# T1 made in GLA's loop, the last quarter summed block by block in the attention, and another order of the output projection's products, PSUM chains and transfers

## The chip, the cores and the metric

The kernel runs on one core of one Trainium2 chip. The metric is the device time of one execution in microseconds; the median of three runs of the kernel before is 1924.75 us (1923.8 to 1924.92). Lower is better. Inputs and outputs are float32.

## What is computed

The reference is one decoder layer over 1024 tokens of width 1024, batch 1, followed by a final norm:

```python
x = x + 0.5 * swiglu_ffn(rmsnorm(x, ffn1_norm), ...)     # width 2816
x = x + hybrid_mixer(rmsnorm(x, mix_norm), w_in, ...)
x = x + 0.5 * swiglu_ffn(rmsnorm(x, ffn2_norm), ...)
return rmsnorm(x, final_norm)
```

The mixer makes one combined projection of the normed tokens and splits its columns between two groups of heads:

```python
o_nsa = nsa_attention(q, ...)          # 8 softmax heads: compressed, selected, window branches, gated
log_a = log_sigmoid(ga @ w_a2 + b_a) / GLA_TAU
o_gla = gla_attention(gq, gk, gv, log_a)     # 4 heads of gated linear attention, in chunks
o_gla = rmsnorm(o_gla, gla_g) * silu(gr)
return concatenate([o_nsa, o_gla], axis=-1) @ w_out
```

Only the way from `o_nsa` and `o_gla` to the product with `w_out`, and the addition of that product to x, is touched by the change.

## The kernel before

**Numbers.** Every large product is made from pairs: an operand is split into a rounded part and the rest, and `mm3` (L211 to L213) issues three matmuls for one product, high by high, high by low and low by high. Splitting takes one ScalarE copy (L206, L239) and one VectorE subtraction (L207, L248).

**Order.** The order of the work is written out by hand. Each engine runs its own list in program order, and so do the DMA queues: nearly all transfers are issued by SP, in the order of the program. Work beside the products is written as generators in `self.side`; `tick()` (L64) advances the first of them by one step, or fetches one pair of weights if some are owed (`later`). `block` (L945) is one product of four k tiles, twelve matmuls, with a tick behind each k tile. `fetch` takes a raw tile that a transfer on SP has filled (`raws`; three raw tiles) and lets ScalarE copy its high part; `settle` lets VectorE subtract.

**The mixer's stages** in the profiled execution: the combined projection until about 778 us; GLA's loop from 778 to 871; queries, keys and the scores of the compressed branch until 985; the attention until 1181; the output projection until 1272; then the second FFN.

**GLA's loop** (`gla`) has 8 iterations of 128 tokens. In each, `tm` issues the products of the gate's columns, `update`, `inter` and L1187 the products of the chunk. `finish(i)` then squares the chunk's output (L1119, ScalarE), reduces it (L1121), makes 1/rms (L1124 on GpSimd) and scales it (L1127, VectorE), which reads the two PSUM banks that L1187 of the next iteration writes. `out(i - 1)` transposes the block before (L1135, TensorE), copies it to a tile "hf" (L1138), stores it to the DRAM tensor gl (L1140), and for the second half of the tokens splits it (L206, L207) and stores both parts to og[1] (L1145). `out` stands ahead of `finish` in each iteration. There are two tiles "hf", which other work uses too: L1287 copies each finished query product into one, and stores it to DRAM (Qfd) from ScalarE's queue.

**The output projection** is one level of Strassen's scheme in Winograd's form. The columns of `w_out` and the tokens are halved, so that eight quarter products become seven, called 1 to 7, of four output tiles m each. The products' weights are quarters of `w_out` (1, 2, 4) or sums of quarters that the kernel has put into two DRAM tensors, `sums0` and `sums1`, while FFN1 ran (5, 3 and 7 with 6). The operands on the tokens' side are "11" and "12" (attention's rows of the first and second half of the tokens), "22" (GLA's rows of the second half) and four combinations of quarters:

- T1 is GLA's rows of the first half minus those of the second,
- T2 and T3 come from "11" and the GLA quarters,
- T4 comes from "12" and T2.

Before the change, `differences` makes T1 at the attention's start from gl (four loads, four GpSimd subtractions at L1494, four stores to DRAM tensor td) and, when the first half's attention is stored, T2 and T3. "22" is loaded ahead of the attention, and two output tiles of product 1 are computed early, between the attention's first units; `early` and `keep` hold them in PSUM and send them to the DRAM tensor part. In `prepare`, a side generator of the projection, the operands are loaded and split (`eased`, L2038 to L2040): T2 on VectorE, T1 and T3 on GpSimd, and T4 is computed there from "12" (L2020 to L2026).

The loop over `plan` in `run` then issues 26 blocks in the order 1 (two tiles), 3, 6, 5, 7, 2, 4. Products 1, 6 and 5 are added up in the same PSUM bank, and each block's sum is added to x by VectorE (L2368, `add`); `moved` lists sums of the early tiles, which GpSimd adds. x is first loaded from the DRAM tensor xs. `done` squares a finished tile and sends it to DRAM for the second FFN. When the last block of product 7 is added, the first half of the tokens is complete; `second` begins its norm: L276 adds up the squares, L287 is eight small matmuls that sum them over the partitions, L292 to L299 give 1/rms, and L324 scales x. Products 2 and 4 run beside it. `self.away` gives the four pairs of the ring of weights that the projection uses.

The attention runs over 88 units (`units`: query block, group, branch, heads). L1566 on GpSimd multiplies the softmax by the gates, L1587 transposes it on TensorE. `collect` sends each finished block of eight to og and counts it in `stored`.

## Time and profile before

The profiled execution took 1924.24 us, its span is 1922.5 us.

| stage | from to (us) | TensorE busy | granted clock | DMA share |
|---|---|---|---|---|
| GLA's loop, later part | 838 to 872 | 33.67 of 34 | 1.00 | 0.44 |
| start of the queries | 872 to 884 | 12.00 of 12 | 1.00 | 0.93 |
| attention | 985 to 1170 | 182.74 of 185 | 1.00 | 0.44 |
| projection, start | 1181 to 1197 | 15.04 of 16 | 1.00 | 0.94 |
| projection | 1197 to 1212 | 14.49 of 15 | 1.00 | 1.05 |
| projection | 1212 to 1237 | 18.43 of 25 | 0.96 | 0.51 |
| projection | 1237 to 1245 | 5.49 of 8 | 0.50 | 0.22 |
| projection, end | 1255 to 1272 | 17.00 of 17 | 0.99 | 0.48 |

PE is TensorE's matmuls, PEld its weight loads, DVE is VectorE, ACT ScalarE, POOL GpSimd, SP the engine that issues most transfers. A row of the waits reads: engine, bank, line that waited, the releasing instruction, then total us, how often, and the longest. A row of the timeline reads: start, duration, engine, line, operation, tile written and tiles read, and in brackets the idle time before it and what ended it. The table of stretches gives the busy time of each engine with the number of instructions, then the granted clock, the mean share of 16 DMA engines in use and GB/s; busy time is counted from records, some of which overlap.

### The profile page before, as it was taken

The page shows a single profiled execution, that of the slowest core. Times are in us where ns is not written, and L with a number is a line of the kernel's source. Part 1 is how long each engine was busy: PE and PEld are TensorE (multiplying, and loading weights), DVE is VectorE, ACT ScalarE, POOL GpSimd, SP SyncE. Part 2 cuts the span into 40 slices and gives each one's busy share as a digit, 9 for nine tenths or more (in the row PEclk, how much of TensorE's full clock was granted, in tenths as well). Part 3 has the DMA queues.
Part 4 walks back from the last instruction along what each step waited for, and adds up shares of the span by engine and source line. Part 5 has one row for each costly group of instructions (what it writes and reads, how often), then busy time and mean ns, then how long its engine had stood idle before and what let it go on. Part 6 is the DMA issues. An engine that isn't in the chain of part 4 may idle for free.

```text
span 1922.5 us, 26555 instructions
## 1 busy us (share of the span) xinstructions
PE 1891.8 (98%) x9243; PEld 1556.8 (81%) x9243; DVE 1414.3 (74%) x2319; ACT 898.8 (47%) x1723; POOL 283.3 (15%) x325
## 2 busy tenths in 40 slices
PE   9999999999999999999999999899999999999998
PEld 7888888888888888778887887678888888888887
DVE  7977778888876761554778887876777777767766
ACT  6633333344544551333488886345433333344343
POOL 0000000033000010121455752600000000000001
PEclk9999999999999999999999999899999999999999
DMA  7434455679964230129474525544333455688652
GB/s 261 154 130 142 141 187 213 225 273 387 376 219 157 88 109 20 44 62 264 159 240 121 173 72 177 199 160 171 116 125 126 154 197 197 217 295 299 233 172 88
DMA packets 182518, 343.37 MB, mean 179 GB/s; under 512 B 18640, under 2 KB 50512, under 8 KB 181872
## 3 DMA queue, kind: packets, MB, share of 16 engines
q1 hardware_dynamic: 171504, 318.31, 48.2%
q0 software_dynamic: 5024, 18.62, 2.7%
q10 hardware_dynamic: 5856, 4.75, 0.8%
q8 instruction: 73, 1.20, 0.3%
q14 instruction: 61, 0.50, 0.1%
HBM read 245.63 MB, written 100.20 MB: 180 GB/s over the span
## 4 chain that ended last, share of the span: by engine, by line
PE 89%; DVE 4%; DMA 2%; issue 1%; POOL 1%; ACT 1%; SPq 0%; ACTq 0%; POOLq 0%; DVEq 0%
PE bank L211 24%; PE bank L213 24%; PE bank L212 24%; PE pair L1468 3%; PE bank L1587 3%; PE bank L990 2%; PE bank L992 2%; PE bank L991 2%; PE bank L1605 1%; PE bank L1606 1%; DMA t<-td 1%; DVE w L248 1%; DMA raw<-gl 1%; PE pair L1476 0%; PE bank L1187 0%
## 5 line engine op out<-in xcount | busy, mean ns | idle before, releaser
L211 PE MATMUL bank<-T,wt 128*128 128x512 f32 x704 | 273.9, 389 | 0.0
L212 PE MATMUL bank<-T,wt 128*128 128x512 f32 x704 | 273.9, 389 | 0.0
L213 PE MATMUL bank<-T,wt 128*128 128x512 f32 x704 | 273.9, 389 | 0.0
L211 PE MATMUL bank<-bd,wd 128*128 128x512 f32 (+1 forms) x632 | 243.0, 385 | 0.0
L213 PE MATMUL bank<-bd,wd 128*128 128x512 f32 (+1 forms) x632 | 242.5, 384 | 0.0
L212 PE MATMUL bank<-bd,wd 128*128 128x512 f32 (+1 forms) x632 | 242.5, 384 | 0.0
L211 PE MATMUL bank<-h,wt 128*128 128x512 f32 x536 | 210.4, 393 | 2.3 <-ACT wt L455 2.3
L213 PE MATMUL bank<-h,wt 128*128 128x512 f32 x536 | 209.0, 390 | 0.1
L212 PE MATMUL bank<-h,wt 128*128 128x512 f32 x536 | 208.8, 390 | 0.0
L636 ACT ACTIVATE g<-bank 128x512 f32<-128x512 f32 x88 | 52.6, 598 | 224.5 <-PE bank L213 222.3
L211 PEld LDWEIGHTS bank<-T,wt 128*128 128x128 f32 x704 | 132.2, 188 | 27.5
L212 PEld LDWEIGHTS bank<-T,wt 128*128 128x128 f32 x704 | 132.2, 188 | 27.4
L213 PEld LDWEIGHTS bank<-T,wt 128*128 128x128 f32 x704 | 132.2, 188 | 27.3
L455 ACT ACTIVATE wt<-v 128x512 fp32r<-128x512 f32 x176 | 109.9, 624 | 84.9 <-PE bank L213 66.9
L213 PEld LDWEIGHTS bank<-bd,wd 128*128 128x128 f32 x632 | 118.8, 188 | 23.6
L212 PEld LDWEIGHTS bank<-bd,wd 128*128 128x128 f32 x632 | 118.8, 188 | 23.2
L211 PEld LDWEIGHTS bank<-bd,wd 128*128 128x128 f32 x632 | 118.8, 188 | 23.2
L294 POOL TENSOR_TENSOR r<-v,mhalf 128x4 f32<-128x4 f32 (+1 forms) x9 | 9.7, 1078 | 856.6 <-DVE v L292 856.6
L458 DVE TENSOR_TENSOR wt<-v,wt 128x512 fp32r<-128x512 f32 x176 | 121.8, 692 | 5.9 <-ACT wt L455 5.9
L211 PEld LDWEIGHTS bank<-h,wt 128*128 128x128 f32 x536 | 100.8, 188 | 24.6 <-ACT wt L455 4.3
L213 PEld LDWEIGHTS bank<-h,wt 128*128 128x128 f32 x536 | 100.7, 188 | 22.5 <-DVE wt L458 1.6
L406 DVE TENSOR_TENSOR bd<-in,bd 128x512 fp32r<-128x512 f32 x154 | 110.7, 720 | 10.8 <-ACT bd L748 10.8
(307 smaller groups left out, 4022.5 us busy)
## 6 DMA issues: line engine op xcount, KB each, us to landing
in<-in_w_f_dram SPq DMA_DIRECT2D x132, 256.0 KB, 5.5
in<-b SPq DMA_DIRECT2D x132, 256.0 KB, 6.0
raw<-in_w_f_dram SPq DMA_DIRECT2D x44, 512.0 KB, 4.4
up<-in_w_f_dram SPq DMA_DIRECT2D x44, 512.0 KB, 5.2
raw<-in_w_in_dram SPq DMA_DIRECT2D x23, 512.0 KB, 4.1
raw<-in_w_f_dram SPq DMA_DIRECT2D x44, 256.0 KB, 4.0
b<-g SPq DMA_DIRECT2D x44, 256.0 KB, 2.0
l<-tb SPq DMA_DIRECT2D x22, 512.0 KB, 5.7
```

The lines of the kernel that those rows point to most:

```text
L211: mm(ps, w[0], x[0], start=first, stop=False, skip_group_check=True)
L212: mm(ps, w[0], x[1], start=False, stop=False, skip_group_check=True)
L213: mm(ps, w[1], x[0], start=False, stop=last, skip_group_check=True)
L406: minus = lambda o, p, q: nc.vector.tensor_tensor(o, p, q, OP.subtract)
L455: nc.scalar.activation(t[:, 0], a, AF.Copy)
L458: nc.vector.tensor_tensor(t[:, 1], a, t[:, 0].bitcast(F32), OP.subtract)
L636: nc.scalar.activation(dst, src, AF.Copy)
L990: mm(p, a, w[:, 0, c], start=f, stop=False, skip_group_check=True)
L991: mm(p, a, w[:, 1, c], start=False, stop=False, skip_group_check=True)
L992: mm(p, b, w[:, 0, c], start=False, stop=l, skip_group_check=True)
L1468: nc.tensor.matmul(s[:, i + c, :w], Q[:, j, r], kk[br, g][:, k0:k0 + w], start=(j == 0 and i % per == 0), stop=False, skip_group_check=True)
L1587: nc.tensor.transpose(t[:, r * 128:r * 128 + 128], heads[r][:, k * 128:k * 128 + 128], self.ident)
```

## The change

- In GLA's loop, from the fifth chunk on, the block of the first half that belongs to it is loaded back from gl (`recall`, into a tile "hf"). `out` subtracts the new block from it (VectorE), takes the high part (ScalarE) and the low part (VectorE) and stores both to a new DRAM tensor, t1d. This stands behind the stores of `ot` and ahead of `finish`.
- The early tiles before and in the attention are now those of product 5 (T1 with `sums0`), in place of product 1; T1 is loaded there as a finished pair. "22" is loaded at the attention's seventh unit into fresh tiles, and all four tiles of product 1 are computed first in the projection.
- `differences` loses its T1 part. When T2 and T3 are stored, it makes, for each query block 4 to 7, "12" and T4 in unsplit form as the block is finished: three loads, two sums on GpSimd (1.28 us is what one of the removed ones, L1494, took), two stores. Block 7's part runs on GpSimd's queue, beside the projection.
- In the projection the order becomes 1, 6, 5 (two tiles), 3, 7, 2, 4. Products 1, 6, 5 and 3 are chained in one PSUM bank per tile, 7 and 4 in another. VectorE has 28 sums into x in place of 34, GpSimd 4 in place of 8. T2 is eased ahead of the loop; T1 comes finished; T3, "12" and T4 are loaded and eased by VectorE. The number of blocks stays 26.
- The ring of weights in the projection uses its usual six pairs; the weights' steps `later` come at odd n and at n = 4 and 8, `ahead` at n = 15, 17, 19; the first half's norm uses bank 3, and its stores to xs go to GpSimd's queue.

```diff
...
                 for s in range(2):
                     nc.sync.dma_start(og_dram[1][:, s, 4:8, ts],
                                       ot[:, s].bitcast(F32).rearrange("p (h t) -> p h t", h=4))
+                d = past.pop()
+                nc.vector.tensor_tensor(d, d, f, OP.subtract)
+                hi = work.tile([128, 512], R32, name="th", bufs=1)
+                self.split(hi, d.bitcast(R32), d)
+                for s, t in enumerate((hi.bitcast(F32), d)):
+                    nc.sync.dma_start(t1[:, s, :, ts], t.rearrange("p (h t) -> p h t", h=4))
+
+        def recall(i):
+            past.append(self.nt.tile([128, 512], F32, name="hf"))
+            nc.sync.dma_start(past[0].rearrange("p (h t) -> p h t", h=4), gl[:, 0, :, i % 4 * 128:i % 4 * 128 + 128])
 
...
             if og is not None:
                 out(i - 1, og, [t[:, 2:] for t in o4])
             og = finish(i, o, sg)
+            if i > 3:
+                recall(i)
         self.later(4)
         yield
         out(7, og, [self.one_bank(3).rearrange("p (h t) -> p h t", h=4)])
...
-    def differences(self, h, og, gl, td, there):
+    def differences(self, h, og, gl, td, stored):
 
...
+        while sum(stored[:4]) < 8:
+            yield
         for k in range(4):
-            r = both(k)
-            for _ in range(2):
-                yield
-            pool.tensor_tensor(r[:, 0], r[:, 0], r[:, 1], OP.subtract)
-            yield
-            nc.sync.dma_start(td[0, :, k], r[:, 0])
-        while not there():
-            yield
-        for k in range(4):
-            nc.sync.dma_start(h[k].bitcast(F32), og[:, :, k])
+            nc.sync.dma_start(h[k].bitcast(F32), og[0][:, :, k])
...
             pool.tensor_tensor(r[:, 1], r[:, 0], r[:, 1], OP.add)
             yield
             for i in range(2):
-                nc.sync.dma_start(td[1 + i, :, k], r[:, i])
+                nc.sync.dma_start(td[i, :, k], r[:, i])
             yield
...
+        stored[8] = 1
+        for b in range(4, 8):
+            while stored[b] < 2:
+                yield
+            queue = nc.sync if b < 7 else pool
+            ts = slice(b % 4 * 128, b % 4 * 128 + 128)
+            a, c, e = [self.nt.tile([128, 512], F32, name="hf") for _ in range(2)] + \
+                [self.nt.tile([128, 512], F32, name="acc", bufs=1)]
+            of = lambda t: t.rearrange("p (k t) -> p k t", k=4)
+            for i, t in enumerate((a, c)):
+                queue.dma_start(of(t), og[1][:, i, :4, ts])
+            queue.dma_start(of(e), td[1, :, :, ts])
+            for _ in range(3):
+                yield
+            pool.tensor_tensor(a, a, c, OP.add)
+            yield
+            yield
+            pool.tensor_tensor(e, a, e, OP.subtract)
+            yield
+            for i, t in enumerate((a, e)):
+                queue.dma_start(td[2 + i, :, :, ts], of(t))
+            yield
+
...
-                stored[0] += half == 0
+                stored[b] += 1
...
                 if (b, g, br, rs[0]) == (*ORDER[-2], 1, 0):
-                    assert not joins
+                    assert stored[8]
                     self.weights(self.wproj)
-                    self.away = {i: i % 4 for i in range(len(self.wproj))}
                     self.owed = 0
                     self.raws(0)
                 if n == len(units) - WF:
                     self.fetch()
                 elif n > len(units) - WF:
                     self.settle()
-                if n > 5:
-                    first_half()
+                first_half()
+                if n == 6:
+                    self.free(*more)
+                    h[1].extend(self.take("T", "h") for _ in range(4))
+                    for k, t in enumerate(h[1]):
+                        nc.sync.dma_start(t.bitcast(F32), og_dram[1][:, :, 4 + k])
...
                     more.append([self.nt.tile([128, 512], F32, name="hf") for _ in range(2)])
                     for m, t in enumerate(more[1]):
-                        nc.sync.dma_start(t, ins["w_out"][m, :, 512:])
+                        nc.sync.dma_start(t, self.sums[0][m, :, 0])
...
-        t = {"12": many(4, "h")}
+        t = {"T2": many(4, "t2")}
+
+        def place(q, i):
+            for k in range(4):
+                nc.sync.dma_start(t[q][k][:, 1].bitcast(F32), td[i, :, k])
+
+        place("T2", 1)
+        self.raws(1)
         x = new_x()
 
         def load(half, k, n=2):
             ts = slice(half * 512, half * 512 + 512)
             nc.sync.dma_start(x[:, k:k + n, ts], xs[:, k:k + n, ts])
 
-        self.raws(1)
-        load(1, 2)
-        part2 = self.take("A", "part", F32)
-        nc.sync.dma_start(part2, part)
-        load(0, 0)
-        load(0, 2)
-        whole = many(2, "t2f", F32)
-        for i in range(2):
-            nc.sync.dma_start(whole[i], td[2, :, 2 * i:2 * i + 2])
-        t["T2"], t["T1"] = many(4, "t2"), many(4, "t1")
+        for half, k in ((1, 0), (1, 2), (1, 4), (1, 6)):
+            load(half, k)
         while ends:
             if self.wnext < 3:
                 self.fetch(1)
             step_ends()
-        self.fetch(4 - self.wnext)
-
-        def place(q, i):
+        self.fetch(3 - self.wnext)
+        self.settle()
+        for k in range(4):
+            for _ in self.eased(t["T2"][k], None, nc.vector):
+                pass
+        B["T2"] = t["T2"]
+        part2 = self.take("A", "part", F32)
+
+        def prepare():
+            yield
+            next(joins)
+            for _ in range(9):
+                yield
+            B["T1"] = many(4, "t1")
             for k in range(4):
-                nc.sync.dma_start(t[q][k][:, 1].bitcast(F32), td[i, :, k])
-
-        def prepare():
-            for k in range(4):
-                yield from self.eased(t["T2"][k], whole[k // 2][:, k % 2], nc.vector)
-            B["T2"] = t["T2"]
-            place("T1", 0)
-            load(1, 4)
-            load(1, 6)
+                nc.sync.dma_start(B["T1"][k].bitcast(F32), t1[:, :, k])
+            nc.sync.dma_start(part2, part)
             load(0, 4)
             load(0, 6)
-            for _ in range(4):
+            for _ in joins:
                 yield
-            for k in range(4):
-                yield from self.eased(t["T1"][k], None, nc.gpsimd)
-            B["T1"], t["T3"] = t["T1"], many(4, "t3")
-            place("T3", 1)
-            for k in range(4):
-                nc.sync.dma_start(t["12"][k].bitcast(F32), og[1][:, :, k])
-            load(1, 0)
             for _ in range(8):
                 yield
-            for k in range(4):
-                yield from self.eased(t["T3"][k], None, nc.gpsimd)
-            B["T3"] = t["T3"]
...
+            load(0, 0)
+            load(0, 2)
+            t["T3"] = many(4, "t3")
+            place("T3", 0)
+            for q, i in (("12", 2), ("T4", 3)):
+                while self.room("TA") < 4:
+                    yield
+                t[q] = many(4, "h")
+                place(q, i)
+            for q in ("T3", "12", "T4"):
+                for _ in range(4):
+                    yield
+                for k in range(4):
+                    yield from self.eased(t[q][k], None, nc.vector)
+                B[q] = t[q]
 
...
-        self.wproj = of(w, 1)[1:] + of2(1, 0) + of2(1, 1) + of2(0, 0) + of2(0, 1) + of(w, 0) + of(w[4:], 0)
+        self.wproj = of(w, 1) + of2(1, 1) + of2(0, 0)[1:] + of2(1, 0) + of2(0, 1) + of(w, 0) + of(w[4:], 0)
...
-                nc.sync.dma_start(xs[:, ks, halves[half]], x[:, ks, halves[half]])
-
-        plan = [(1, 2), (1, 3)] + [(q, m) for q in (3, 6, 5, 7, 2, 4) for m in range(4)]
-        with_, X, turn = {1: "22", 3: "11", 6: "T2", 5: "T1", 7: "T3", 2: "12", 4: "T4"}, {2: bank}, 0
-        moved = {6: (0, 0), 7: (0, 1), 8: (1, 4), 9: (1, 5), 10: (0, 4), 11: (0, 5), 14: (1, 0), 15: (1, 1)}
+                (nc.sync if half else nc.gpsimd).dma_start(xs[:, ks, halves[half]], x[:, ks, halves[half]])
+
+        plan = [(q, m) for q in (1, 6, 5, 3, 7, 2, 4) for m in range(2 * (q == 5), 4)]
+        with_, X, Y = {1: "22", 3: "11", 6: "T2", 5: "T1", 7: "T3", 2: "12", 4: "T4"}, {0: bank}, {}
+        moved = {6: (0, 4), 7: (0, 5), 8: (0, 0), 9: (0, 1)}
         for n, (q, m) in enumerate(plan):
-            for _ in range(999):
-                if with_[q] in M:
-                    break
+            while with_[q] not in M:
                 self.tick()
...
+            if q == 1 and m:
+                X[m] = self.one_bank((2, 0, 1, 3)[m])
+            elif q == 7:
+                Y[m] = self.one_bank(4 + m)
+            p = self.one_bank((2, 0, 1)[m % 3]) if q == 2 else Y[m] if q in (7, 4) else X[m]
+            self.block(p, n // 2, n % 2, M[with_[q]], range(2, 4) if n == 0 else range(4), q in (1, 7, 2), True)
+            add({1: 1, 6: 1, 5: 0, 3: 0, 7: 0, 2: 1, 4: 1}[q], m + 4 * (q in (6, 5, 7, 4)), p)
+            if n in (6, 7):
+                add(0, n - 2, X[n - 6])
             if n in moved:
                 half, k = moved[n]
                 add(half, k, part[:, k % 4], nc.gpsimd)
-            if n % 2:
+            if q in (3, 7, 2, 4):
+                done(int(q in (2, 4)), m + 4 * (q in (7, 4)))
+            if n % 2 or n in (4, 8):
                 self.later(1)
...
-            if n in (20, 21, 22):
-                ahead(n - 20)
+            if n in (15, 17, 19):
+                ahead((n - 15) // 2)
...
```

More of the change, by code (lines that the diff above doesn't have):

```diff
@@ L1028, in gates_and_decays, with gla @@
         yield
-    def gla(self, h, qk, la, gv, wr, og_dram, gl, one, work):
+    def gla(self, h, qk, la, gv, wr, og_dram, gl, t1, one, work):
         nc, tc, ins = self.nc, self.tc, self.ins
@@ L1160, in lead @@
             yield
-        D, og = {}, None
+        D, og, past = {}, None, []
         self.side.append(lead())
@@ L1526, in differences, with attention @@
             yield
-    def attention(self, queries, Q, pcd, K1, K2, V, og_dram, h, masks, first, early, keep, gl, td):
+        stored[8] = 1
[20 more added lines that the diff above has]
+            yield
+    def attention(self, queries, Q, pcd, K1, K2, V, og_dram, h, masks, first, early, keep, gl, td, more):
         nc, tc, ins, gates, Vc = self.nc, self.tc, self.ins, self.gates, self.Vc
@@ L1569, in attention @@
             mm = nc.tensor.matmul
-            late, slot, stored = [], [0], [0]
+            late, slot, stored = [], [0], [0] * 9
             def flush(keep=0):
@@ L1622, in collect @@
                                   f[s * 64:s * 64 + 64].rearrange("p (r t) -> p r t", r=4))
-                stored[0] += half == 0
+                stored[b] += 1
             ends, res = [], {}
-            joins = [self.differences(h[0], og_dram[0], gl, td, lambda: stored[0] == 8)]
+            joins = [self.differences(h[0], og_dram, gl, td, stored)]
             units = [(b, g, br, rs) for b, g in ORDER for br in (1, 0)
@@ L1724, in attention @@
             flush()
-        return step_ends, ends, bank
+        return step_ends, ends, bank, joins[0]
     def mixer(self, x, h, w, free_x, new_x):
@@ L1733, in mixer @@
         gl = self.dram.tile([128, 2, 4, 512], F32, name="gl")
-        td = self.dram.tile([3, 128, 4, 512], F32, name="td")
+        td = self.dram.tile([4, 128, 4, 512], F32, name="td")
+        t1 = self.dram.tile([128, 2, 4, 512], F32, name="t1d")
         c0 = ExitStack()
@@ L1796, in mixer @@
             gv = gq.tile([128, 8, 512], F32, name="gv")
-            gla = self.gla(h, qk, la, gv, w + 11, og, gl, gq, work)
+            gla = self.gla(h, qk, la, gv, w + 11, og, gl, t1, gq, work)
             next(gla)
@@ L1956, in mixer @@
                 slot[1] = "T"
-            B = {"11": [self.take("T", "h") for _ in range(4)], "22": more[0]}
-            step_ends, ends, bank = self.attention(queries, Q, pcd, K1, K2, V, og, (B["11"], B["22"]), masks, first,
-                                                   early, keep, gl, td)
+            B = {"11": [self.take("T", "h") for _ in range(4)], "22": []}
+            step_ends, ends, bank, joins = self.attention(queries, Q, pcd, K1, K2, V, og, (B["11"], B["22"]), masks,
+                                                          first, early, keep, gl, td, more[0])
         c0.close()
@@ L2013, in prepare @@
-            B["T3"] = t["T3"]
-            while self.room("TA") < 4:
-                yield
-            t["T4"] = many(4, "t4")
-            for k in range(4):
-                b, t4, f = t["12"][k], t["T4"][k], self.nt.tile([128, 512], F32, name="hf")
-                hi, lo = [b[:, s] for s in range(2)]
-                nc.gpsimd.tensor_tensor(f, hi.bitcast(F32), lo.bitcast(F32), OP.add)
-                yield
-                yield
-                nc.scalar.activation(hi, f, AF.Copy)
-                nc.gpsimd.tensor_tensor(whole[k // 2][:, k % 2], f, whole[k // 2][:, k % 2], OP.subtract)
-                yield
-                nc.vector.tensor_tensor(lo, f, hi.bitcast(F32), OP.subtract)
-                yield
-                yield from self.eased(t4, whole[k // 2][:, k % 2], nc.vector)
@@ L2029, in prepare @@
-            self.free(*whole)
-            B.update({q: t[q] for q in ("12", "T4")})
+            load(0, 0)
[13 more added lines that the diff above has]
+                B[q] = t[q]
@@ L2057, in free_x @@
             st[0].close()
-        sums = [self.dram.tile([4, 128, 2, 512], F32, name=f"sums{i}") for i in range(2)]
+        sums = self.sums = [self.dram.tile([4, 128, 2, 512], F32, name=f"sums{i}") for i in range(2)]
         w = ins["w_out"]
@@ L2276, in second @@
                         yield
-                for n, _ in enumerate(self.norm(ns3[half], x, hg, 2, half, 6 + half, True, 2, 1 + 1.4 * half,
+                for n, _ in enumerate(self.norm(ns3[half], x, hg, 2, half, 3 + 4 * half, True, 2, 1 + 1.4 * half,
                                                 1 - half, 2 if half else 5, range(KT) if half else EARLY)):
@@ L2406, in run @@
                 self.free(*M.pop(with_[q]))
-            if n == 15:
+            if n == 11:
                 self.free(part)
```

18 lines of the change are left out of this document (1 added, 17 removed).

## The prediction

> **What bounds the kernel now.** I read the page's first rows, then the list of what TensorE waited for, then the table of stretches, and last the timeline where that list points.
>
> ```profile
> span 1922.5 us, 26555 instructions
> PE 1891.8 (98%) x9243; PEld 1556.8 (81%) x9243; DVE 1414.3 (74%) x2319; ACT 898.8 (47%) x1723; POOL 283.3 (15%) x325
> ```
>
> TensorE is busy for 1891.8 of 1922.5 us, and the change leaves its matmuls as many as they were (the output projection keeps its 26 blocks). So the time can move only through what TensorE waits for, and through its clock. The waits, as total, times and longest:
>
> ```profile
> PE bank L211 <- DVE x L2368: 10.5, 2, 9.1
> PE bank L287 <- DVE acc L276: 2.2, 2, 1.5
> PE bank L1587 <- POOL p L1566: 1.2, 2, 0.8
> PE pair L1349 <- DMA q<-Qfd: 0.2, 1, 0.2
> ```
>
> ```profile
> core 0: us, PE busy (x) PEld busy (x) DVE busy (x) ACT busy (x) POOL busy (x), PEclk, DMA share, GB/s
> 838.00:872.00 34.00, 33.67 (x199) 25.95 (x198) 18.28 (x39) 11.36 (x26) 9.29 (x10) 1.00 0.44 124
> 985.00:1170.00 185.00, 182.74 (x1162) 147.10 (x1161) 153.99 (x281) 150.38 (x340) 111.00 (x122) 1.00 0.44 126
> 1181.00:1197.00 16.00, 15.04 (x67) 12.08 (x65) 10.11 (x17) 7.78 (x14) 1.34 (x2) 1.00 0.94 321
> 1197.00:1212.00 15.00, 14.49 (x64) 12.02 (x65) 11.78 (x14) 8.38 (x16) 11.80 (x9) 1.00 1.05 387
> 1237.00:1245.00 8.00, 5.49 (x13) 4.34 (x14) 7.92 (x14) 3.34 (x6) 0.12 (x1) 0.50 0.22 77
> 1250.00:1255.00 5.00, 4.17 (x16) 3.46 (x17) 2.14 (x5) 0.63 (x1) 1.05 (x1) 0.71 0.00 0
> ```
>
> Two things show. The loop of GLA (838 to 872) has almost no gap on TensorE, so whatever is made late there is paid in full. The output projection (1181 to 1272) has the stall of 9.1 us, and twice a lower clock behind it; its first 31 us run with the DMA engines full.
>
> ```profile
> 1197.51 0.47 PE L211 MATMUL bank<-h,w 128*128 128x512 f32 x1 [1.47 <-DVE x L2368]
> 1200.35 0.39 PE L211 MATMUL bank<-t,w 128*128 128x512 f32 x1
> ...
> 1239.51 0.80 PE L211 MATMUL bank<-t,w 128*128 128x512 f32 x1 [9.08 <-DVE x L2368]
> ...
> 1244.80 0.60 PE L211 MATMUL bank<-h,w 128*128 128x512 f32 x1
> ...
> 1250.83 1.05 PE L287 MATMUL bank<-ones,acc 128*128 128x1 f32 x8 [1.53 <-DVE acc L276]
> ```
>
> At full clock a block's 12 matmuls start 0.227 us apart (2.72 us a block: 12 matmuls from 1197.51 to 1200.35, the first one slow). Behind the long stall 12 of them take 5.29 us (1239.51 to 1244.80), 2.6 us too many; in the 5 us from L287 on, at a clock of 0.71, I count 1.8 us. All that the projection can give back is therefore 1.47 + 9.08 + 2.6 + 1.53 + 1.8 = 16.5 us.
>
> **GLA's loop: adds, on the path.** From the fifth chunk on, out(i) now also subtracts (DVE), rounds (ACT) and takes the low part (DVE), ahead of finish(i) on both engines, and sends two stores and one load of 256 KB on SP.
>
> ```profile
> 840.18 0.63 ACT L206 ACTIVATE ot<-hf 128x512 fp32r<-128x512 f32 x1
> 840.84 1.06 DVE L207 TENSOR_TENSOR ot<-hf,ot 128x512 fp32r<-128x512 f32 x1
> 841.83 0.67 DVE L1121 TENSOR_REDUCE ss<-acc 128x4 f32<-128x512 f32 x1
> ...
> 854.87 1.12 DVE L1127 SCALAR_TENSOR_TENSOR sq<-bank,ss,sg 128x128 f32<-128x128 f32 x4 [1.12 <-POOL ss L1124]
> 855.88 1.16 PE L1187 MATMUL bank<-gv,A 128*128 128x128 f32 x8
> ```
>
> L1127 reads the banks that L1187 of the next iteration writes. TensorE starts L1187 at 855.88, in the last of the four scalings that began at 854.87 and take 1.12: it arrives just when the bank comes free. Ahead of L1121 the DVE now has, after ot's low part, the subtraction (0.6; its nearest row is an add of this shape, L2368 further below, 0.68 on average), the wait for the rounding on ACT (0.63, as L206), and the low part (0.69, as L207 below). That is 1.9 us, and with a hand-over the reduction, which stood right behind the low part (840.84 + 1.06 = 841.90), comes 2.0 us later; the squares that it sums stand behind the same rounding on ACT. It comes in finish(5), finish(6) and finish(7). The first two hold L1187 of iterations 6 and 7: 2.0 and, less 0.15 of slack, 1.85. The third holds the bank of the second query product:
>
> ```profile
> 864.53 1.12 DVE L1127 SCALAR_TENSOR_TENSOR sq<-bank,ss,sg 128x128 f32<-128x128 f32 x4 [1.12 <-POOL ss L1124]
> 865.72 0.40 PE L211 MATMUL bank<-h,w 128*128 128x512 f32 x1
> ```
>
> It starts about when L1127 ends (865.65): 1.8. Together 5.65 us. Bounds: 0 if DVE is so far ahead that the order does not matter (the waits for POOL's L1124 in these rows are DVE idle time, but it lies behind L1121, so it doesn't help), and 3 x 2.6 = 7.8 if ot's low part takes 1.06 and the new one too.
>
> **Queries: the same edit, a buffer and a queue.** The recalled block sits in a tile "hf", of which there are two, and the last one is freed when its store to t1 has landed.
>
> ```profile
> 863.04 6.57 SPq L224 DMA_DIRECT2D raw<-in_w_in_dram  x4
> 871.56 1.15 ACT L239 ACTIVATE w<-raw 128x512 fp32r<-128x512 f32 x2 [3.26 <-DMA raw<-in_w_in_dram]
> 872.62 0.58 ACT L1138 ACTIVATE hf<-bank 128x512 f32<-128x512 f32 x1
> 873.77 0.58 ACT L1287 ACTIVATE hf<-bank 128x512 f32<-128x512 f32 x1
> 873.90 0.69 DVE L207 TENSOR_TENSOR ot<-hf,ot 128x512 fp32r<-128x512 f32 x1 [0.38 <-ACT ot L206]
> 877.10 0.39 PE L211 MATMUL bank<-h,w 128*128 128x512 f32 x1
> gl<-hf SPq DMA_DIRECT2D x5, 256.0 KB, 2.3
> Qfd<-hf ACTq DMA_DIRECT2D x7, 256.0 KB, 4.5
> ```
>
> In the times of before (that is, without the two waits that move everything): the load of the last recalled block stands on SP ahead of the weights' loads at 863.04, and waits until the block before it has been stored and its tile is free; I put the weights' loads 4.6 us later (stores of 2.3 us behind a chain 2 us later). ACT, which already waited 3.26 us for them, copies at 873.6 instead of 871.56, and out(7)'s copy (0.58) runs at 874.75 instead of 872.62. From its end at 875.3 come rounding 0.63, low part 0.69, subtraction 0.6, rounding 0.63, low part 0.69, so the store leaves at 878.75 and lands 2.3 later, at 881.1. L1287 at 873.77 needs that tile: it ends at 881.85. The query product at 877.10 writes the bank that L1287 reads; it is due at 878.9 with the 1.8 above, so it waits 3.0 us. Bounds 0 (loads no later and a store of less than 2 us) and 5 (the weights' copies late for TensorE as well). The tokens' copies Qfd go out behind on ACT's queue, and loads of them come back for L1349, where TensorE waited 0.2 us: each lands in 4.5 us on full DMA engines. I take 1 us, between 0 and 3. **Sum up to here: 5.65 + 3.0 + 1 = 9.7 us lost.**
>
> **Attention: removes little.** Four loads, four subtractions on POOL and four stores at its start go; POOL's multiplications queue behind them.
>
> ```profile
> 994.10 1.28 POOL L1494 TENSOR_TENSOR raw<-raw 128x512 f32<-128x512 f32 x1 [2.51 <-DMA raw<-gl]
> 995.37 3.90 POOL L1566 TENSOR_SCALAR p<-p,rd,gates 128x384 f32<-128x384 f32 x6
> ```
>
> POOL stood 2.51 us at 994 with six multiplications behind it; that is the 1.2 us of L1587 in the list of waits, and they go: 1.2 gained. For each of the blocks 4 to 7 POOL gets two sums of 1.28 us and SP five transfers of 256 KB. POOL is busy for 111 of 185 us and the DMA engines for 0.44 of this stretch, and each sum has several units of the loop until it is wanted: I take 0 (bounds -1 to 2; without that cover 8 x 1.28 = 10 us of POOL would show at L1587). Loading "22" (2 MB) at the sixth unit lies under the same 0.44.
>
> **Projection: the cause of its stall goes, its transfers grow.** First the sums of the whole stage (count, busy time, mean in ns, idle time), then one pair of weight subtractions at two places, then the loads of operands with their landing time:
>
> ```profile
> L2368 DVE TENSOR_TENSOR x<-x,bank 128x512 f32<-128x512 f32 x29 | 19.3, 678 | 7.0 <-PE bank L213 6.9
> 1212.03 3.42 DVE L248 TENSOR_TENSOR w<-raw,w 128x512 fp32r<-128x512 f32 x2
> 1242.53 1.29 DVE L248 TENSOR_TENSOR w<-raw,w 128x512 fp32r<-128x512 f32 x2
> t<-td SPq DMA_DIRECT2D x8, 256.0 KB, 7.6
> ```
>
> Two weight subtractions took 3.42 us while POOL worked beside them and 1.29 later. The change takes POOL's work on the operands away and half of its eight x sums, and leaves all easing to DVE, with six of the 34 sums fewer. Up to the rms of the first half DVE has 20 weight subtractions, 20 sums, 16 easings and 7 squares' sums of 0.65 (half of 1.29): some 41 us in the 66 from 1184 to 1250. DVE itself no longer sets the pace.
>
> The transfers may. On SP, up to the operands of the last product and the pair of weights behind them, in units of 512 KB: T2 2, weights 1 to 3 3, x 8, T1 (now both parts) 4, part 1, block 7's sums 2.5, T3 2, "12" 2, T4 2, six weights more 6, together 32.5 or 17.0 MB. At the 354 GB/s that 1181 to 1212 moved (the mean of 321 and 387) they take 48 us, from 1183 to 1231. DVE takes its list in order, so what waits for a late tile holds the sums behind it. Behind T4's landing stand its four easings (2.7 us), four sums of product 7 and their squares (8 x 0.65 = 5.2) and four weight subtractions (2.6): 10.5 us, 1241.5, with no hand-over in it. The squares' last sum allowed L287 to start at 1250.83 before. I take 1245.5, about halfway: a gain of 5.3 us. The slow matmuls behind L287 stay. The long stall does not vanish then, it shrinks and moves to the product-5 block, whose bank waits for DVE, and to L287. Bounds: a gain of 16.5 (all transfers in time), a loss of 4 (each tile one landing of 7.6 later than now, less half of it covered).
>
> The clock after short waits: 1.47 us idle left 1.00 and 1.53 us with eight tiny matmuls 0.71, so for the new waits of 2 to 3 us I take full clock, and up to 1.8 us each for the upper end. The Trainium skill ("TensorE: Matmul & The Clock Gate", Part 1, The HAM clock gate) has the clock halved only after an idle window of about 3.4 us; by it these waits cost nothing more, and the 0.71 behind a gap of 1.53 us would not have been there, so here the trace speaks against it.
>
> **Sum:** 1924.24 (the profiled execution: span 1922.5 and 1.74 around it) + 9.7 - 1.2 - 5.3 = 1927.4. That execution lies 0.5 below the median of 1924.75, so I say **1928.0**.
>
> **Rivals.** *Faster: the projection flows.* If T1, ready from DRAM since GLA's loop, and the chains of four products in one bank leave DVE early enough, nearly all of the 16.5 us comes back, and with 9.7 lost and 1.2 gained the time is 1916.7. For it speaks DVE's 41 us of work in 66; against it the DMA share of 0.94 and 1.05, with more bytes to come. *The loop costs little.* If the extra load does not hold the weights' loads (a tile free in time), 3.0 and 1 fall away: 1924.0. The DMA share of 0.44 in 838 to 872 speaks for it, the two "hf" tiles against it. *Slower: block 7's sums block SP.* In this mechanism the loads of "12" and T4 wait on SP for stores of block 7, which POOL's queue sends late:
>
> ```profile
> og<-sq POOLq DMA_DIRECT2D x2, 128.0 KB, 7.6
> ```
>
> Two such landings one after the other, 7.6 each, are 15 us behind the last attention block; with the sums between them the loads, and every weight queued behind them on SP, come after 1205 instead of 1195. It decides once those loads are issued later than 1200, since the 31 us of full DMA then no longer cover them: the first half ends 4 us after the old 1250.83 and the time is 1924.75 + 9.7 - 1.2 + 4 = 1937. Against it: weights already loaded for the first blocks.
>
> **How the numbers follow.** Forecast 0.42 (1924.5 to 1932 as its own range), the flowing projection 0.27, the cheap loop 0.18, blocked SP 0.13. A measurement tells 0.2% (3.85 us) from nothing: faster is below 1920.9, slower above 1928.6. Of the forecast's 0.42 I count 0.02 as faster, 0.17 as same, 0.23 as slower; of the flowing projection 0.25 faster and 0.02 same; of the cheap loop 0.03 faster, 0.11 same and 0.04 slower; the blocked queue is all slower. That makes 0.30, 0.30 and 0.40. The range runs from 1916, the projection's full gain, to 1936, most of the blocked queue.
>
> **What would show it.** L1187 waits for L1127 about 2 us in two iterations and L211 for it once; L1287 waits for a store to t1 and the product behind it about 3 us; L1587's wait for POOL is gone; the 9.1 us behind L2368 are gone, and L287 or a block of product 5 waits instead, with ACT's weight copies waiting for "sums" between 1200 and 1222. The forecast is wrong if finish's extra 2 us do not appear on TensorE, or if L287 starts more than 9 us earlier or not earlier at all.

## The result and the profile after

The changed kernel takes 1942.46 us (median of 4 runs, 1941.93 to 1944.6) against 1924.84 us: 1.0093 times as long, with a 95% interval of 1.0076 to 1.0111. It is slower, by about 17.6 us; the forecast was 1928.0, in a range up to 1936. First rows of the page after, then what TensorE waited for (total us, times, longest):

```profile
span 1941.0 us, 26480 instructions
PE 1896.8 (98%) x9243; PEld 1560.9 (80%) x9243; DVE 1409.0 (73%) x2325; ACT 898.0 (46%) x1723; POOL 264.4 (14%) x318
```

```profile
PE bank L211 <- ACT w L239: 11.5, 1, 11.5
PE bank L287 <- DVE acc L276: 6.0, 2, 5.3
PE bank L1197 <- DVE sq L1127: 4.3, 2, 2.3
PE bank L211 <- ACT wt L455: 2.5, 4, 1.5
PE bank L211 <- DVE sq L1127: 1.7, 1, 1.7
PE pair L1361 <- DMA q<-Qfd: 1.5, 1, 1.5
PE pair L1358 <- DMA q<-bias: 1.1, 1, 1.1
```

The matmuls are as many as before (9243). L1197 is the old L1187, L1361 the old L1349, L2390 the old L2368, L1299 the old L1287. The long stall is still there (11.5 in place of 9.1), L287 waits longer, and ahead of the attention there are five waits that were 0.3 us or less before. Four rows of TensorE's timeline after cut the span into stages: the last transposes of GLA, the attention's first scores, its last product with V, and the second FFN's start.

```profile
878.72 0.60 PE L1135 MATMUL bank<-ident,sq 128*128 128x128 f32 x4
...
978.30 0.34 PE L1480 MATMUL pair<-K,q 128*128 128x128 f32 x2
...
1196.34 0.39 PE L1633 MATMUL pair<-pt,V 128*128 128x512 f32 x1
...
1291.93 0.50 PE L211 MATMUL bank<-h,wt 128*128 128x512 f32 x1 [1.49 <-ACT wt L455]
```

The same rows of the kernel before stand at 871.19, 965.15, 1183.41 and 1274.10. Subtracted stage by stage, in us:

| kernel | GLA's loop | queries, scores | attention | projection | rest | span |
|---|---|---|---|---|---|---|
| after | +7.5 | +5.6 | -0.2 | +4.9 | +0.7 | +18.5 |
| forecast | +5.65 | +4.0 | -1.2 | -5.3 | 0 | +3.2 |

Where the clock was cut, the table of stretches shows it (us, busy time of the five engines, granted clock, DMA share, GB/s):

```profile
846.90:849.90 3.00, 2.95 (x16) 2.44 (x16) 1.56 (x4) 0.38 (x1) 0.00 (x0) 0.52 0.12 36
861.50:864.50 3.00, 3.00 (x22) 2.44 (x22) 0.89 (x3) 0.00 (x0) 0.00 (x0) 1.00 0.15 43
905.70:912.00 6.30, 6.28 (x19) 5.32 (x20) 1.69 (x3) 0.63 (x1) 0.00 (x0) 0.51 0.96 289
1215.00:1230.00 15.00, 3.54 (x13) 2.59 (x12) 5.72 (x9) 2.30 (x4) 3.38 (x4) 0.75 1.05 392
```

The first wait of GLA (2.32 us) left half the clock for 3 us, the second (1.98) left it whole, and the pair of short waits at the first scores (1.07 and 1.49) halved it for 6 us, about 3 us lost. In the projection the DMA engines are full while TensorE stands (1.05 in the last row).

**The stall of 11.5 us.** VectorE's timeline, then TensorE's:

```profile
1213.92 2.80 DVE L248 TENSOR_TENSOR w<-raw,w 128x512 fp32r<-128x512 f32 x2 [1.53 <-ACT w L239]
1216.64 0.67 DVE L2390 TENSOR_TENSOR x<-x,bank 128x512 f32<-128x512 f32 x1
1226.60 1.29 DVE L248 TENSOR_TENSOR w<-raw,w 128x512 fp32r<-128x512 f32 x2 [9.28 <-ACT w L239]
1227.81 2.47 DVE L2390 TENSOR_TENSOR x<-x,bank 128x512 f32<-128x512 f32 x4
```

```profile
1216.74 0.39 PE L213 MATMUL bank<-t,w 128*128 128x512 f32 x1
1228.59 0.77 PE L211 MATMUL bank<-t,w 128*128 128x512 f32 x1 [11.46 <-ACT w L239]
```

The matmul at 1228.59 is the first of product 5. It continues the chain in a bank that VectorE must have read for product 6, and the first of the four sums at 1227.81 ends when it starts. The sum stood 9.28 us behind a weight subtraction, that one behind ScalarE's copy, and the copy behind its transfer:

```profile
1225.93 1.15 ACT L239 ACTIVATE w<-raw 128x512 fp32r<-128x512 f32 x2 [11.53 <-DMA raw<-sums]
```

The row of the matmul names ScalarE because a copy for a later pair ended at the same moment; the experiment later_odd shows that VectorE's list was the cause. T1, the block's other operand, was there: its last load left at 1205.8 and landed after 13.7 us, at 1219.5.

### The profile page after: what moved, and what is told of

It reads as the page before. It is cut to its first block, busy times and chain, and to the rows that moved or that the text cites. A ratio compares the mean times of both kernels' runs of the same rounds, so it can differ in the third digit from the quotient of the medians.

```text
span 1941.0 us, 26480 instructions
## 1 busy us (share of the span) xinstructions
PE 1896.8 (98%) x9243; PEld 1560.9 (80%) x9243; DVE 1409.0 (73%) x2325; ACT 898.0 (46%) x1723; POOL 264.4 (14%) x318
## 4 chain that ended last, share of the span: by engine, by line
PE 87%; DVE 4%; DMA 4%; ACT 2%; issue 2%; POOL 0%; SPq 0%; ACTq 0%; POOLq 0%; DVEq 0%
PE bank L211 23%; PE bank L213 23%; PE bank L212 23%; PE pair L1480 3%; PE bank L1614 3%; PE bank L990 2%; PE bank L992 2%; PE bank L991 2%; PE bank L1632 1%; DMA raw<-sums 1%; PE bank L1633 1%; PE bank L1197 0%; DVE w L248 0%; PE pair L1488 0%; DMA Qfd<-hf 0%
## 5 line engine op out<-in xcount | busy, mean ns | idle before, releaser
L211 PE MATMUL bank<-T,wt 128*128 128x512 f32 x704 | 273.9, 389 | 0.0
L211 PE MATMUL bank<-bd,wd 128*128 128x512 f32 (+1 forms) x632 | 243.0, 385 | 0.0
L211 PE MATMUL bank<-h,wt 128*128 128x512 f32 x536 | 210.1, 392 | 2.5 <-ACT wt L455 2.5
L211 PEld LDWEIGHTS bank<-T,wt 128*128 128x128 f32 x704 | 132.2, 188 | 27.6
L211 PEld LDWEIGHTS bank<-bd,wd 128*128 128x128 f32 x632 | 118.8, 188 | 22.9
L211 PEld LDWEIGHTS bank<-h,wt 128*128 128x128 f32 x536 | 100.7, 188 | 24.5 <-ACT wt L455 4.1
L213 PEld LDWEIGHTS bank<-h,wt 128*128 128x128 f32 x536 | 100.6, 188 | 22.6 <-DVE wt L458 1.8
L212 PEld LDWEIGHTS bank<-h,wt 128*128 128x128 f32 x536 | 100.7, 188 | 20.5
```

Of the source, the lines that this page charges most:

```text
L211: mm(ps, w[0], x[0], start=first, stop=False, skip_group_check=True)
L212: mm(ps, w[0], x[1], start=False, stop=False, skip_group_check=True)
L213: mm(ps, w[1], x[0], start=False, stop=last, skip_group_check=True)
```

## The experiments

Medians are compared with runs of the kernel before on the same chip; stages are from each profile, in us against before (table at the end of this section). A profile is one execution, so its stages add up to within some 4 us of what the medians say.

**gla_only** puts GLA's part into the kernel before, with nothing else:

```diff
+                d = past.pop()
+                nc.vector.tensor_tensor(d, d, f, OP.subtract)
...
+            if i > 3:
+                recall(i)
```

> The kernel before with one edit alone: the recall, the subtraction, the split and the two stores to t1 in GLA's loop, ahead of finish; t1 is never read. Theory A (the edit is paid in full, three waits of 2 us, a slow clock behind them, and later loads at the first scores): about 1938 us, 13 more than before, all of it before the attention starts. Theory B (the 13 us before the attention come partly from other parts of the change, such as the other early product and its loads): at most 1932.

1939.17 us, ratio 1.0067 (1.0052 to 1.0082): 13.8 more. Ahead of the attention it loses 12.6, with the same waits as after and nearly the same lengths. Theory A holds for that part. Another 3.2 us are lost in the attention, which after does not lose and theory A did not name; 1.6 of them are waits of TensorE for GpSimd's multiplications (2.8 in place of 1.2), the rest stays open. Its clock fell behind the second wait, where after's was whole:

```profile
847.10:850.10 3.00, 2.94 (x18) 2.42 (x19) 1.56 (x4) 0.38 (x1) 0.00 (x0) 0.69 0.09 26
861.70:864.70 3.00, 2.94 (x17) 2.41 (x17) 0.95 (x3) 0.00 (x0) 0.00 (x0) 0.53 0.16 48
```

**no_diff** takes the recall and the computation out of after and leaves two stores a block; **no_t1** takes those out as well, and loads GLA's rows of the second half in T1's place:

```diff
-                d = past.pop()
...
+                for s in range(2):
+                    nc.sync.dma_start(t1[:, s, :, ts], ot[:, s]...)    # in no_diff only
```

> The kernel after, without recall, subtraction, rounding and low part in GLA's loop; t1 gets the split block itself, so T1 is not the difference and the output is another one. Theory A: about 1929.5 us (1942.5 less 13), what is left being the projection's 5 us. Theory B: 1934 or more, since the other parts keep their share of the 13.

> no_diff without the stores to t1 as well: T1's tiles are loaded from GLA's rows of the second half, so that the output is another one. Theory W (the 2.7 us that no_diff still loses at the first scores are transfers: two more stores of 256 KB a block at a time of full DMA engines): nothing is lost before the attention, 1929. Theory V (they come from other loads of the change): the first scores start as late as in no_diff, 1931.4.

no_diff: 1931.37 us, ratio 1.0032 (1.0021 to 1.0043), no new wait in GLA's loop, 2.7 lost at the first scores. no_t1: 1929.89, ratio 1.0026 (1.0015 to 1.0037), ahead of the attention 0.2 from before. The two waits of no_diff that no_t1 does not have:

```profile
896.61 0.47 PE L1353 MATMUL pair<-q,ident_r 128*128 128x512 f32 x1 [1.42 <-DMA q<-bias]
898.11 0.71 PE L1356 MATMUL pair<-Kc,q 128*128 128x128 f32 x4 [1.02 <-DMA q<-Qfd]
```

Theory W holds: the stores alone, without any arithmetic, make the first scores late. Of what they still lose, 4.0 and 3.9 us are the projection's; no_t1 also loses 1.8 in the attention, where a wait of 2.4 us for a copy on ScalarE is new; what made that late I did not follow.

**diff_last** moves the difference behind finish; **own_last** also gives the last recalled block a tile of its own; **pool_q** also moves recall and stores to GpSimd's queue:

```diff
+            rest = out(i - 1, og, [t[:, 2:] for t in o4])
             og = finish(i, o, sg)
+            if rest: rest()
...
+            past.append(work.tile(..., name="sg") if i == 7 else self.nt.tile(..., name="hf"))   # own_last
...
-                        nc.sync.dma_start(t1[:, s, :, ts], ...)                                  # pool_q
+                        nc.gpsimd.dma_start(t1[:, s, :, ts], ...)
```

> The kernel after, with the subtraction, the split and the stores of the difference behind finish in the list of each engine; the same computation. Theory A with the order of the list as cause of the waits: L1127 is no later than before, the three waits of 2 us and the slow clock behind them go, 1942.5 - 7.5 = 1935; the loads of the queries' weights still stand behind the recall, so the 5.6 us at the first scores stay. Theory C (VectorE has no room for the added work wherever it stands): within 2 us of 1942.5, another wait in place of L1197's.

> diff_last, with the last recalled block in the tile of the gate (free after the last finish) in place of a third user of the two tiles hf; the same computation. Theory H (the 3.5 us that diff_last still loses at the second product of the queries are the wait of L1304's copy for the tile hf that the store to t1 holds): that wait goes, 3 to 4 us less than diff_last, and what is left before the attention is the late loads at the first scores, 2 to 3 us. Theory S (SP is what is late: the weights' loads stand behind the recall): the wait moves to the weights or to L211 behind ACT's copies, less than 1 us gained.

> own_last, with the recall and the two stores to t1 issued on GpSimd's queue in place of SP's; the same computation. Theory S (the queries' weights' loads stand on SP behind the stores and the recall, which wait for VectorE; in own_last they leave at 869.5 in place of 863.0): they leave before 865, the wait of L211 for L1305's copy goes, and the time before the attention is 2 to 3 us above the kernel before instead of 6.3: 3 to 4 us less than own_last, 1932 to 1934. Theory H' (the late copy is ScalarE's list, with the rounding of the difference in it): the wait stays above 2 us.

diff_last: 1938.76 us (1934.98 to 1939.64), ratio 1.0063 (1.0048 to 1.0078). The three waits in the loop are gone, so their cause was the order of the lists; 7.1 us of GLA's loss go, but one wait comes behind (3.5 us, L211 for the copy L1304), and 6.9 us stay lost ahead of the attention. The profiled execution is the fastest of the four; the median lies 3.8 above the 1935 that theory A gave. own_last: 1936.55, ratio 1.0056 (1.0041 to 1.0071); the wait shrinks from 3.5 to 2.8 only, and in all3 below, whose loop is the same, it is 3.3, so the tile was a small part of it at most and theory H does not hold. pool_q: 1939.69, ratio 1.0075 (1.0061 to 1.0088), where theory S gave 1932 to 1934. The first weights' load of the queries (SP's queue), first in own_last, then in pool_q:

```profile
869.50 6.90 SPq L224 DMA_DIRECT2D raw<-in_w_in_dram  x4
```

```profile
865.03 8.59 SPq L224 DMA_DIRECT2D raw<-in_w_in_dram  x4
```

```profile
PE pair L1364 <- DMA q<-bias: 2.0, 1, 2.0
PE bank L211 <- DVE sq L1127: 1.2, 1, 1.2
```

The loads leave 4.5 us earlier and the wait for the copy (L1305 here, L1299 in after) falls to 0.7 us, as theory S said; yet nothing is gained. In place of it pool_q waits for the loads of the biases and, in the loop, for L1127 again. In this stretch the DMA engines are nearly full whatever the order (0.93 of them already before the change, from 872 to 884), so I take it that what T1 moves there is paid. For the two stores no_diff and no_t1 show it; for the whole it is an estimate: the last two blocks bring 2 x 768 KB, 1.6 MB, at the 289 GB/s of the row above 5.4 us; 6.3 to 8.8 were lost in these three kernels, and 2.7 with two thirds of the bytes.

**later_odd, t4_late and x_first** change the projection's order in after:

```diff
-            if n % 2 or n in (4, 8):
+            if n % 2:                                      # all three
...
-            for q in ("T3", "12", "T4"):
+            for q in ("T3", "12"):                         # t4_late: T4 eased behind L287
...
-        for half, k in ((1, 0), (1, 2), (1, 4), (1, 6)):
+        for half, k in ((1, 0), (1, 2), (1, 4), (0, 4), (1, 6)):     # x_first
```

> The kernel after, with the two extra steps of weights (n = 4 and 8) taken out, so that pairs 6 and on are fetched later in the order. Theory P (the 11.5 us at the first block of product 5 are VectorE's sum of its bank, standing in VectorE's list behind the low part of weight pair 6, which waits for its transfer): the sum no longer stands behind it, 6 to 11 us less, 1932 to 1936. Theory Q (the transfers are simply full, and T1 or the block's own weights are not there): no gain, 1941 to 1945.

> later_odd, with T4's four easings issued behind L287 in place of ahead of the first half's last sums. Theory D (the first half's sum is now late by VectorE's list and its hand-overs with ScalarE, of which T4's easings are a part of about 5 us): L287 waits some 3 us in place of 8.0, and the time is about 1932. Theory Q (the transfers set it): L287 waits as long, 1937.

> later_odd, with the load of x's tiles 4 and 5 of the first half ahead of T1's. Theory D: the sums at product 6 no longer wait 6.1 us for x, the 4.3 us at product 5 go, but as the first half's sum is set by VectorE's list further on, L287 waits 3 to 4 us longer: 1936 to 1937.5, the same as later_odd. Theory E (each wait is a loss by itself): 4 us less, 1933.

later_odd: 1937.13 us, ratio 1.0057 (1.004 to 1.0074). Its waits, and the sum that product 5 now waits for:

```profile
PE bank L287 <- DVE acc L276: 8.7, 2, 8.0
PE bank L211 <- DVE x L2390: 4.3, 1, 4.3
```

```profile
1223.89 1.88 DVE L2390 TENSOR_TENSOR x<-x,bank 128x512 f32<-128x512 f32 x3 [6.10 <-DMA x<-xs]
```

Theory P holds: with the pairs fetched later, 11.5 us become 4.3, behind x's own load. Of these 7.2 us 2.7 come back at L287 (5.3 to 8.0), which theory P did not count, so the time is 1.1 us above its 1936. t4_late: 1933.28, ratio 1.0042 (1.0027 to 1.0057); L287 waits 3.8, and the projection takes 86.2 us against before's 90.7. That is theory D, and the 4.5 us are nearly the gain of the forecast. x_first: 1937.84, ratio 1.0064 (1.0049 to 1.0079), not told apart from later_odd: its sums no longer wait for x, but two other blocks wait 2.4 and 2.2 us, by the timeline each until a sum of VectorE ends, and L287 waits 8.9. That is theory D again, not E.

**all3** is own_last with the three edits of the projection, **best1** pool_q with two of them (without x_first).

> own_last with the three edits of the projection (later_odd, t4_late, x_first) together. Theories H and D: ahead of the attention 2.5 us lost, the attention 0, the projection some 4 us shorter than before's 90.7: 1923 to 1925. If the transfers set the end of the first half (Q): 1929 or more.

> pool_q with the two edits of the projection of t4_late. From t4_late's projection (86.2 us against before's 90.7) and theory S: 1924.8 + 2.5 - 0.2 - 4.5 = 1922.6. If theory S is wrong: 1926.

1929.72 us, ratio 1.0025 (1.0015 to 1.0034), and 1931.85, ratio 1.0036 (1.0023 to 1.0048). Both are better than after and worse than before, and both miss what was expected (1923 to 1925, and 1922.6 or 1926): GLA's part keeps 6.5 and 8.6 us where 2.5 were counted, and the projection gains 2.0 and 3.0 in place of t4_late's 4.5. all3's time is one that theory Q allowed, but its projection is shorter than before's, so it does not speak for Q.

**order_only** keeps the change's projection with t4_late's edits, and has T1 and the early tiles of product 1 as in the kernel before, so that GpSimd again has eight sums; **order_dve4** and **order_dve8** then move sums of the early tiles from GpSimd to VectorE, four behind L287, then all eight:

```diff
-        moved = {..., 14: (1, 0), 15: (1, 1), 16: (1, 4), 17: (1, 5)}
+        moved = {..., 18: (1, 0), 19: (1, 1), 22: (1, 4), 23: (1, 5)}
...
-                add(half, k, part[:, k % 4], nc.gpsimd)
+                add(half, k, part[:, k % 4], nc.vector)       # dve4: only where half is 1
```

> The change's projection (chains 1, 6, 5, 3 and 7, 4 in one bank, sums per block in the attention, T3, 12 and T4 eased by VectorE) with the two edits of t4_late, but GLA's loop, T1's making and the early tiles of product 1 as in the kernel before; T1 is loaded unsplit (1 MB less) and eased by VectorE, GpSimd has eight sums of early tiles again. Theory D and W (GLA's part is a pure loss, the projection's order alone is a gain once T4's easings and the extra weight steps are out of the way): nothing lost before the attention, 4.5 us gained in the projection, 1920.5. Theory Q (the transfers set the projection's pace, so that T1 ahead of time was needed for it): no gain in the projection, 1925 or more.

> order_only, with the four sums of early tiles into the second half on VectorE behind the first half's last sum, in place of GpSimd ahead of it. Theory G (VectorE is slowed by GpSimd's sums: pairs of weight subtractions of 3.48 and 3.42 us in place of 1.29): L287 waits 4 us less, 8.7 to 4.5, and with the slow clock behind it the time is 1924 to 1925. Theory Q (late transfers of T1 and of the weights set the first half's end): L287 waits as long, 1928 to 1929.

> order_dve4, with the other four sums of early tiles on VectorE too. Theory G: the subtraction of 6.33 us at 1212 becomes 1.29 and four sums of 0.68 are added, L287 waits 2 us less again, 1922 to 1923. Theory Q: as order_only, 1928 to 1929.

order_only: 1929.13 us, ratio 1.0022 (1.0013 to 1.0031): nothing lost ahead of the attention, as theory W wants, but the projection is 1.5 us longer, so theory D's 1920.5 is missed by 8.6. One pair of subtractions of it beside three sums on GpSimd, and the same pair in order_dve8:

```profile
1212.55 6.33 DVE L248 TENSOR_TENSOR w<-raw,w 128x512 fp32r<-128x512 f32 x2
1214.38 3.94 POOL L2392 TENSOR_TENSOR x<-x,part 128x512 f32<-128x512 f32 x3
```

```profile
1214.59 1.29 DVE L248 TENSOR_TENSOR w<-raw,w 128x512 fp32r<-128x512 f32 x2
...
PE bank L287 <- DVE acc L276: 2.5, 1, 2.5
```

order_dve4: 1927.63, ratio 1.0007 (0.9999 to 1.0016), not told from before and 2.6 above what theory G gave; L287 waits 5.8 in place of 8.7, and the two later pairs of subtractions that stood beside GpSimd's sums take 1.30 and 1.29 us in place of 3.48 and 3.42. Here four sums changed both engine and place; in order_dve8 the other four change the engine alone: **1922.86 us**, ratio 0.9985 (0.9976 to 0.9994); L287 waits 2.5. It is the only kernel here that beats both, by 0.15% of before. Theory G holds: GpSimd's sums slowed VectorE, and T1's early making had bought four fewer of them. The kernel before with its own eight sums on VectorE was not run, so how much of the gain over before is the new order and how much the moved sums stays open. In the profiled execution order_dve8 waits 4.3 us for ScalarE at the second FFN's start (1.9 before), at the end of the projection's column below, and the clock is 0.50 for 5 us behind it, which is its 2.3 us of rest.

| kernel | to the attention | attention | projection | rest |
|---|---|---|---|---|
| after | +13.1 | -0.2 | +4.9 | +0.7 |
| gla_only | +12.6 | +3.2 | -0.1 | -0.1 |
| no_diff | +2.7 | +0.4 | +4.0 | +0.7 |
| no_t1 | +0.2 | +1.8 | +3.9 | +1.3 |
| diff_last | +6.9 | -0.9 | +4.0 | +0.7 |
| own_last | +6.3 | -0.1 | +5.4 | +0.6 |
| pool_q | +8.8 | +0.7 | +4.2 | +1.7 |
| later_odd | +13.2 | +0.1 | +1.1 | +0.7 |
| t4_late | +12.0 | -1.2 | -4.5 | +1.3 |
| x_first | +13.0 | -0.6 | +1.0 | +0.7 |
| all3 | +6.5 | -0.8 | -2.0 | +1.3 |
| best1 | +8.6 | -0.6 | -3.0 | +1.7 |
| order_only | -0.1 | +0.7 | +1.5 | +1.3 |
| order_dve4 | -0.1 | +2.9 | +0.2 | +1.5 |
| order_dve8 | -0.3 | +0.7 | -4.2 | +2.3 |

## Why the prediction was wrong

**GLA's loop: right, the clock left out.** L1121 stands where it was put, 2.1 us later, and the waits are the three forecast (2.0, 1.85 and 1.8 there):

```profile
846.95 1.99 PE L1197 MATMUL bank<-gv,A 128*128 128x128 f32 x8 [2.32 <-DVE sq L1127]
...
861.50 1.16 PE L1197 MATMUL bank<-gv,A 128*128 128x128 f32 x8 [1.98 <-DVE sq L1127]
...
873.15 0.47 PE L211 MATMUL bank<-h,w 128*128 128x512 f32 x1 [1.66 <-DVE sq L1127]
```

The loop lost 7.5 in place of 5.65. The step that failed is "for the new waits of 2 to 3 us I take full clock": the first wait cost about 1.5 us more. The upper end named there, 1.8 us each, would have held it.

**Queries: the size nearly right by luck, the place wrong.** L1299's copy did wait for the store to t1, as forecast:

```profile
887.25 0.60 ACT L1299 ACTIVATE hf<-bank 128x512 f32<-128x512 f32 x1 [1.94 <-DMA t1d<-hf]
```

But it was the second copy; the first came just in time for its bank, and TensorE did not wait the 3.0 us there. The weights' loads, put 4.6 us later, left 8.2 later (871.24 against 863.04), of which 5.6 are the loop's own waits and 2.6 the recall. The loss came at the first scores, where I had put 1 us between 0 and 3: waits of 1.07 and 1.49 (0.2 before) and half a clock behind them, 5.6 in all. The term that was mis-sized is that 1 us: I had the tokens' copies late on full DMA engines, and did not price the clock. When diff_last took the loop's own waits away, the forecast wait for the copy did appear on TensorE (3.5 us).

**Attention: -0.2 in place of -1.2.** L1566's wait at L1587 went, as forecast; 0.2 to 0.4 us at each of three other places came instead.

**Projection: the sign was wrong, and this decided it.** The count of bytes was right: in the 48 us from 1196 to 1244 the DMA engines moved 17.2 MB (358 GB/s, a share of 0.99), as the forecast had it, 13 us earlier, from 1183 to 1231. What failed is the step "I take 1245.5, about halfway: a gain of 5.3 us". It put the lateness of the transfers at the end of the half alone. But pair 6 of the weights, wanted at the thirteenth block, was fetched so early in the lists that VectorE stood behind its transfer with the sum that the ninth block's bank needed. The text said that the stall moves to this block, and gave it no price of its own: it was 11.5 us, above the 9.1 it replaced, and the bound of 4 us lost was too near as well (4.9). L287, which the forecast put 5.3 us earlier, came 3.0 later: 1253.8 in the times of before, that is, less the 12.9 us by which the attention ended later. "Not earlier at all" was one of its signs of being wrong.

```profile
1266.73 1.87 PE L287 MATMUL bank<-ones,acc 128*128 128x1 f32 x8 [5.35 <-DVE acc L276]
```

later_odd and t4_late show both halves of it: two edits of the order, and the projection is 4.5 us shorter than before, with the same transfers. So the capacity that the forecast counted was there, but not in the written order. (Its 1.8 us behind L287 in the kernel before are 1.45 by the row that it shows, 5 us at 0.71; that changes little.)

The rival of block 7's sums blocking SP is not what happened, though the loads of "12" and T4 left at 1227.3, later than its limit of 1200 (1213 in the times of after). The last sum was done at 1216.2, the two stores landed by 1223.0, 4 us before these loads, and no wait of SP for them shows: the loads stood behind x and T3 in SP's list. The transfer that VectorE stood behind had been issued at 1213.3, ahead of all of them.

```profile
1214.59 1.59 POOL L1549 TENSOR_TENSOR acc<-hf,acc 128x512 f32<-128x512 f32 x1
```

**VectorE "no longer sets the pace".** True of its busy time, and no help: its idle time of 9.28 us stood inside its list, ahead of work that TensorE wanted. The relief from GpSimd's work, on the other hand, is real, as order_dve8 shows.

The rest, 0.7 us behind the projection, I did not follow.

## What to carry to other kernels

On engines that run a fixed list, a late transfer delays everything behind its first reader, so price each early fetch by what stands behind it in the reader's list, not by when its data are wanted. In a stretch where TensorE has no slack, even pieces of 0.7 us of work on another engine belong behind the instruction that frees TensorE's bank. Full DMA engines alone do not say what helps: at the first scores an earlier place in the queue gained nothing (pool_q), in the projection, as full, two edits of the order gained 9.4 us (t4_late). When a wait of 2 us is forecast on TensorE, add the clock, here up to 1.5 us, to its upper end.

## What the runs showed of the hardware

Waits of about 2 us do not cost the same each time: 2.32 us idle left a clock of 0.52 in after and 0.69 in gla_only, 1.98 us left 1.00 in after and 2.00 us left 0.53 in gla_only. The Trainium skill ("TensorE: Matmul & The Clock Gate", Part 1, The HAM clock gate) calls the activity window free-running, and these rows agree with that, though none of them shows the window. Its idle window of about 3.4 us, which the forecast weighed, is not what they show, since 2 us were enough.

The loads of 512 KB of weights from "sums" took longer to land in the fuller stretch: 8.0 us in the median before, from 1177 to 1232, and in after, from 1190 to 1245:

```profile
raw<-sums SPq DMA_DIRECT2D x6, 512.0 KB, 11.9
```

And sums on GpSimd beside VectorE, three of them in a row, stretched two subtractions from 1.29 to 6.33 us, more than the 3.42 that the trace before had shown.
